# A two-layer hybrid decoder on one core: fifth product's copy in PSUM, later weights for the first pairs, x let go by halves, mixer products reordered

## Chip, cores and metric

One Trainium2 chip, one core of it. The metric is device time in microseconds (us) of one execution, as the median of several. Engines are named as the profile names them: PE (TensorE, matmul), PEld (its weight loads), DVE (VectorE), ACT (ScalarE), POOL (GpSimd), SP (SyncE, which issues nearly all DMAs here). PEclk is the granted clock of PE as a share of the full one.

## What is computed

All float32, one sequence of 512 tokens, width 1024, two layers. Cut to what the change touches:

```python
def swiglu_ffn(x, w_gu, w_down):                       # w_gu: 1024 x 5632, w_down: 2816 x 1024
    gate, up = jnp.split(x @ w_gu, 2, axis=-1)
    return (jax.nn.silu(gate) * up) @ w_down

def ab_mixer(xn, ...):                                 # layer 0's mixer
    proj = xn @ w_in
    xa, ga, qk, v, o, i_pre, f_pre = jnp.split(proj, cuts, axis=-1)
    ya = gelu(ga) * rglru(causal_dwconv(xa), ...)      # a linear scan over time
    yb = mlstm_block(qk, v, o, i_pre, f_pre, ...)      # 4 heads, 4 chunks of 128 tokens
    return concat([ya, yb]) @ w_out

for i in range(2):
    x = x + 0.5 * swiglu_ffn(rmsnorm(x, ffn1_norm[i]), ...)
    x = x + (ab_mixer if i == 0 else nsa_mixer)(rmsnorm(x, mix_norm[i]), ...)
    x = x + 0.5 * swiglu_ffn(rmsnorm(x, ffn2_norm[i]), ...)
return rmsnorm(x, final_norm)
```

## The kernel before

Six stages follow one another: f0a, ab, f0b, f1a, nsa, f1b (four feed-forward layers, two mixers). Features lie on partitions and the 512 tokens in the free direction. A float32 product is made of three matmuls in a rounded format (`mm3`, L175 to L177): weights and data are each split in a high part (written by ACT) and a low part (by DVE, now and then POOL), and PE does high·high, high·low, low·high. Raw weights come by DMA from SP's queue, which takes its DMAs in order.

**A feed-forward stage** makes 22 column tiles of gate and up. The first four (`CLASSIC`, j = 0 to 3) are done in the plain way, on the normalised input x, 8 slices k of 128 rows by `mm3`. x lies in four blocks: the high parts of k 0 to 3, the high parts of k 4 to 7, and the two blocks of low parts. The other tiles come as pairs (`Pair`): seven products p1 to p7 (each 4 slices, 12 matmuls of 256 columns) of combined weight quarters with combined quarters of x, named B11, Q7, Q6, B21, Q4, Q5, B22, in place of eight. `Quarters.split` makes them (L258 and L261 on ACT, L259 and L262 on DVE). The last four go into the blocks that x held, so their splits wait until the plain tile j = 3 has read x for the last time: `lay` says which quarter lies where. The first two pairs p and q run p.p1, p.p7, p.p6, q.p1, q.p7, p.p2, p.p4, p.p5, q.p6, p.p3, q.p2, q.p4, q.p5 on PE. `Pair.load` asks for four raw weight pieces (L305 to L308), adds them up on DVE (L309 to L311) and splits them (L318 on ACT, L319 on DVE).

Two accumulators a and b of a pair lie in PSUM. ACT copies p1's result into b's first half (L336); p5's is copied to an SBUF tile u4 (L363) and added by DVE (L364).

**What sets the order.** The build gives each instruction a place in its engine's list, and the engine takes the list in order; `tc.high_priority(offset=...)` moves instructions so many places ahead. Pieces of a pair are asked for RAHEAD = 400 places ahead and split SAHEAD = 230 ahead. PE's order in a feed-forward stage is written out by hand (`manual_schedule`).

**The mixer ab** runs four rounds i: projection and convolution for RG-LRU (`rg_conv`, L522 to L525), q and k of the mLSTM, RG-LRU's gate products (`rg_gate`, L539), the output gate; in between the mLSTM's gate rows (`gate_rows`, DVE work on 4 rows) and their transposes (`gate_cols`). Then `rg_scan`: reciprocals (L549), a scan (L554) for each i on DVE. Then v's projection (`proj_tok`), then four chunks of the mLSTM, each with scores in PSUM (L639 and L640), exponentials, and products L662, L664, L671.

Of the kernel before, what the change touches and what calls it, by code (L numbers as in the profile page):

```python
# [7 lines left out]
F32 = mybir.dt.float32  # L8
F32R = mybir.dt.float32r
AF = mybir.ActivationFunctionType  # L10
OP = mybir.AluOpType

P = 128
# [10 lines left out]
AHEAD = 90  # L24
SAHEAD = 230
RAHEAD = 400
EV = 320
H = T // 2
CLASSIC = 4
# [25 lines left out]
def build(tc, a, out, stages=("f0a", "ab", "f0b", "f1a", "nsa", "f1b")):  # L55
    nc = tc.nc
    with ExitStack() as ctx:
# [236 lines left out]
        class Pair:  # L294
# [1 line left out]
            def __init__(self, Q, down):  # L296
                self.Q, self.down, self.W = Q, down, {}

            def load(self, w, rb):
                with tc.high_priority(offset=RAHEAD):  # L300
                    ra, rc = (blk(rb[2 * (turns[1] % 2) + i], F32, f"r{i}")[:, :4 * T]
                              .rearrange("p (s c) -> p s c", s=4) for i in range(2))
                    turns[1] += 1

                    nc.sync.dma_start(ra[:, 0], w[0][:, :T])  # L305
                    nc.sync.dma_start(rc[:, 3], w[1][:, :T])
                    nc.sync.dma_start(ra[:, 3], w[1][:, T:])
                    nc.sync.dma_start(rc[:, 0], w[0][:, T:])  # L308
                    nc.vector.tensor_add(ra[:, 1:3], ra[:, 0:4:3], rc[:, 3:4].to_broadcast([P, 2, T]))  # L309
                    nc.vector.tensor_add(rc[:, 1], ra[:, 0], ra[:, 2])  # L310
                    nc.vector.tensor_add(rc[:, 2], rc[:, 0], rc[:, 1])  # L311
                with tc.high_priority(offset=SAHEAD):
                    for src, names in ((ra[:, 0:2], ("B11", "Q7")), (rc[:, 0:2], ("B21", "Q6")),
                                       (ra[:, 2:4], ("Q5", "Q4")), (rc[:, 2:3], ("B22",))):
                        hi, lo = parts()
                        m = len(names) * T
                        src = src.rearrange("p s c -> p (s c)")
                        nc.scalar.activation(hi[:, :m], src, AF.Copy)  # L318
                        nc.vector.tensor_sub(lo[:, :m], src, hi[:, :m].bitcast(F32))  # L319
                        for n, name in enumerate(names):  # L320
                            self.W[name] = hi[:, n * T:(n + 1) * T], lo[:, n * T:(n + 1) * T]
                return self
# [35 lines left out]

            def p5(self):
                self.product(self.a, "Q5", False)  # L360
                u4 = tp.tile([P, H], F32, name="u4", bufs=1)
                with tc.high_priority(offset=EV):
                    nc.scalar.activation(u4, self.a[:, :H], AF.Copy)  # L363
                    nc.vector.tensor_add(self.t2[:, H:], u4, self.t2[:, H:])  # L364

            def p3(self):
                self.product(self.a, "B22", False)
# [6 lines left out]
        def ffn(gname, wgu, wd, x, lay, nxt, first=None):  # L374
# [30 lines left out]
            for j in range(CLASSIC):  # L405
                (gh, gl), (uh, ul) = first if first and j == 0 else (wload(wgu[j, 0]), wload(wgu[j, 1]))
                pg, pu = psum(), psum2()
                seq = [(k, w) for k in range(KT) for w in range(2)]
                if j:
                    seq.sort(key=lambda e: e[1])  # L410
                with tc.manual_schedule(engines=PE_ONLY):
                    for n, (k, w) in enumerate(seq):
                        ks = slice(k * P, (k + 1) * P)
                        ps, hi, lo = ((pg, gh, gl), (pu, uh, ul))[w]
                        mm3(ps, hi[:, ks], lo[:, ks], x[0][k], x[1][k], k == 0, k == KT - 1)
                        if 16 * j + n == at[0]:
                            rms_sum([acc])
                        if 16 * j + n == at[1]:
                            rms_row()
                wait.append((j, pg, pu))  # L420
                if j == 1:
                    hidden(*wait.pop(0))
                    quarters.norm()
                    hidden(*wait.pop(0))
                    quarters.before()
                if j >= 2:
                    hidden(*wait.pop(0))
# [4 lines left out]
            while j0 < JT:  # L432
                j1 = min(JT, j0 + NH)
                js = list(range(max(CLASSIC, j0), j1))
                with tc.manual_schedule(engines=PE_ONLY):
                    if js[0] == CLASSIC:

                        p, q = (Pair(quarters.Q, downs(j)).load(wgu[j], rb) for j in js[:2])
                        for f in (p.p1, p.p7, p.p6, q.p1, q.p7, p.p2, p.p4, p.p5, q.p6, p.p3, q.p2, q.p4, q.p5):
                            f()  # L440
                        left = [q.p3]
                        js = js[2:]
                    for j in js:
                        p = Pair(quarters.Q, downs(j)).load(wgu[j], rb)
                        end = j == j1 - 1
                        for f in (p.p1, p.p7, *left, p.p6, p.p2, *((p.p5, p.p4, p.p3) if end else (p.p4, p.p5))):
                            f()
                        left = [] if end else [p.p3]
                if j1 == JT:
                    roots(hpart(JT - 1)[0].bitcast(F32))  # L450
                for i in range(KT):
                    ps = psum()
                    hi, lo = wload(wd[i, :, j0 * P:j1 * P], (j1 - j0) * P)
                    for k in range(j1 - j0):
                        mm3(ps, hi[:, k * P:(k + 1) * P], lo[:, k * P:(k + 1) * P], *hpart(k),
                            k == 0, k == j1 - j0 - 1)
                    nc.vector.scalar_tensor_tensor(X[i], ps, 0.5, X[i], op0=OP.mult, op1=OP.add)  # L457
                    if j1 == JT:
                        nxt(i)
                j0 = j1  # L460
# [15 lines left out]
        def ab(x, nxt):  # L476
# [83 lines left out]
            O4 = ones[0:4, 0:1].to_broadcast([4, T])  # L560
            gcol = cp.tile([P, NT, 8], F32, name="gcol")

            def gate_rows():
                ps = fm(x, "ab_fm", 4)
                nc.vector.tensor_mul(LI, ps[0:4], R[0:4])
                nc.vector.tensor_scalar(LI, LI, col("ml_b_i", rows=4), None, op0=OP.add)
                nc.vector.tensor_mul(Z, ps[32:36], R[32:36])
                nc.vector.tensor_scalar(Z, Z, col("ml_b_f", rows=4), None, op0=OP.add)
                nc.vector.scalar_tensor_tensor(E_, Z, -1.0, Z, op0=OP.mult, op1=OP.max)
                nc.scalar.activation(E_, E_, AF.Exp, scale=-1.0)  # L570
                nc.vector.tensor_scalar(Bc, E_, 1.0, None, op0=OP.add)
                nc.scalar.activation(LF, Bc, AF.Ln)
                nc.vector.tensor_scalar(Bc, Bc, -1.0, None, op0=OP.add)
                nc.vector.tensor_sub(E_, E_, Bc)
                nc.vector.tensor_add(LF, LF, E_)
                nc.vector.scalar_tensor_tensor(LF, Z, 0.0, LF, op0=OP.min, op1=OP.subtract)
                nc.vector.tensor_tensor_scan(Bc, O4, LF, 0.0, op0=OP.mult, op1=OP.add)
                nc.vector.tensor_sub(G, LI, Bc)
                nc.vector.tensor_tensor_scan(M, O4, G, -BIG, op0=OP.mult, op1=OP.max)
                nc.vector.tensor_add(EM, Bc, M)  # L580
                nc.scalar.activation(EM, EM, AF.Exp, scale=-1.0)
# [32 lines left out]
                nc.vector.tensor_sub(yal[i], z, yah[i].bitcast(F32))  # L614

            ahead(x, "ab_fm", (4, 0, 5, 9))
            gate_rows()
            for i in range(4):
                rg_conv(i)
                qk(i)  # L620
                qk(4 + i)
                rg_gate(i)
                out_gate(i)
                if i == 1:
                    gate_cols()

            rg_scan()
            pss = proj_tok(a["ab_v"], x)
# [6 lines left out]
            for c in range(NT):  # L635
                cs = slice(c * P, (c + 1) * P)
                pm, pst, pk = psum(), psum(), psum2()
                for h in range(NH):
                    nc.tensor.matmul(h4(pm)[:, h], sel[h], M[:, cs], start=True, stop=True)  # L639
                    nc.tensor.matmul(h4(pst)[:, h], kT[:, h, cs], qT[:, h, cs], start=True, stop=True)  # L640
                Et, Pt, kw, qd = (h4(t[b + c % 2]) for t, b in ((EP, 0), (EP, 2), (KQ, 0), (KQ, 2)))
                nc.vector.tensor_add(Et, h4(pm), mask.unsqueeze(1).to_broadcast([P, NH, P]))
                prev = mlast
# [502 lines left out]
        for n, st in enumerate(stages):  # L1146
# [13 lines left out]
            if st == "ab":  # L1160
                ab(x, nxt)
            elif st == "nsa":
                nsa(x, nxt)
            else:
                f = {"f0a": 0, "f0b": 1, "f1a": 2, "f1b": 3}[st]

                lay = (((4, 5, 6, 0, 1, 2, 3), (7, 8, 9, 10), (13, 14, 15, 16), (11, 12)) if base == 0 else
                       ((14, 15, 16, 4, 5, 6, 7), (2, 3, 0, 1), (8, 9, 10, 11), (12, 13)))
                ffn(plan[st], a["wgu"][f], a["wd"][f], x, lay, nxt, first if n == 0 else None)
            base = nbase  # L1170
            x = xn[0] if xn else None
# [101 lines left out]
```

## Time and profile before

| | |
|---|---|
| runs | 2098.58, 2088.83, 2093.01 us; median 2093.01 |
| the profiled execution | 2106.2 us; span of its records 2104.5 us; mean PEclk 0.976 |
| busy shares | PE 96%, PEld 83%, DVE 66%, ACT 49%, POOL 13% |
| chain that ended last, by engine | PE 72%, DVE 12%, DMA 6%, issue 5%, ACT 3% |

An engine's list is in order, so an instruction that waits holds all behind it. In a timeline row "[2.36 <-ACT qQ L261]" says that the engine sat idle for 2.36 us before the instruction until ACT's line 261, which writes qQ, let it go. A matmul's duration overlaps the next one's: from start to start is what it takes of PE.

### The profile page before, as it was taken

The page shows a single profiled execution, that of the slowest core. Times are in us where ns is not written, and L with a number is a line of the kernel's source. Part 1 is how long each engine was busy: PE and PEld are TensorE (multiplying, and loading weights), DVE is VectorE, ACT ScalarE, POOL GpSimd, SP SyncE. Part 2 cuts the span into 40 slices and gives each one's busy share as a digit, 9 for nine tenths or more (in the row PEclk, how much of TensorE's full clock was granted, in tenths as well). Part 3 has the DMA queues.
Part 4 walks back from the last instruction along what each step waited for, and adds up shares of the span by engine and source line. Part 5 has one row for each costly group of instructions (what it writes and reads, how often), then busy time and mean ns, then how long its engine had stood idle before and what let it go on. Part 6 is the DMA issues. An engine that isn't in the chain of part 4 may idle for free.

```text
span 2104.5 us, 30561 instructions
## 1 busy us (share of the span) xinstructions
PE 2014.4 (96%) x11896; PEld 1750.7 (83%) x11896; DVE 1383.4 (66%) x2189; ACT 1027.8 (49%) x1900; POOL 280.0 (13%) x290
## 2 busy tenths in 40 slices
PE   7999899989999999999999999999999999999997
PEld 5889898767888998897889989877777677999896
DVE  6847647488568657475865747433777788657474
ACT  4525436445445435254544525424877755435252
POOL 3000000243020000002000000201646440000002
PEclk9999999999899999999999999999999999999998
DMA  5232322222132323233232323321000032323212
GB/s 172 74 115 83 111 85 76 90 81 90 61 101 80 109 82 111 76 98 108 79 113 83 107 88 99 121 90 60 31 21 17 31 106 80 102 89 111 85 61 85
DMA packets 74737, 182.10 MB, mean 87 GB/s; under 512 B 8416, under 2 KB 9184, under 8 KB 74592
## 3 DMA queue, kind: packets, MB, share of 16 engines
q1 hardware_dynamic: 74448, 180.06, 27.6%
q8 instruction: 93, 1.52, 0.3%
q14 instruction: 52, 0.43, 0.1%
q10 hardware_dynamic: 144, 0.09, 0.0%
HBM read 178.02 MB, written 2.10 MB: 86 GB/s over the span
## 4 chain that ended last, share of the span: by engine, by line
PE 72%; DVE 12%; DMA 6%; issue 5%; ACT 3%; POOL 0%; SPq 0%; DVEq 0%; POOLq 0%; ACTq 0%
PE ps L175 17%; PE ps L176 17%; PE ps L177 17%; DMA r<-wgu 6%; PE pt L176 3%; PE pt L175 3%; PE pt L177 3%; PE px L984 2%; PE pt L779 2%; DVE wlo L319 1%; PE pt L1000 1%; DVE wx L319 1%; DVE r L309 1%; DVE r L310 1%; PE ps L944 1%
## 5 line engine op out<-in xcount | busy, mean ns | idle before, releaser
L169 ACT ACTIVATE whi<-raw 128x1024 fp32r<-128x1024 f32 (+2 forms) x196 | 193.3, 988 | 374.4 <-PE ps L176 254.5
L176 PE MATMUL ps<-h,whi 128*128 128x512 f32 x704 | 278.9, 396 | 0.7 <-DVE h L390 0.7
L175 PE MATMUL ps<-h,whi 128*128 128x512 f32 x704 | 277.8, 395 | 0.7 <-ACT h L389 0.7
L177 PE MATMUL ps<-h,wlo 128*128 128x512 f32 x704 | 277.2, 394 | 0.0
L318 ACT ACTIVATE whi<-r 128x1024 fp32r<-128x1024 f32 (+1 forms) x174 | 165.8, 953 | 211.2 <-PE ps L176 171.0
L170 DVE TENSOR_TENSOR wlo<-raw,whi 128x1024 fp32r<-128x1024 f32 (+2 forms) x166 | 192.5, 1162 | 78.7 <-ACT whi L169 73.8
L116 POOL TENSOR_TENSOR acc<-acc,t 128x512 f32<-128x512 f32 x48 | 76.9, 1603 | 1149.4 <-ACT t L114 1144.2
L457 DVE SCALAR_TENSOR_TENSOR X<-ps,X 128x512 f32<-128x512 f32 x96 | 66.4, 691 | 238.1 <-PE ps L177 238.1
L319 DVE TENSOR_TENSOR wlo<-r,whi 128x1024 fp32r<-128x1024 f32 (+1 forms) x174 | 189.1, 1088 | 28.1 <-ACT whi L318 27.8
L175 PE MATMUL ps<-x,whi 128*128 128x512 f32 x432 | 179.4, 415 | 6.0 <-ACT whi L1133 6.0
L176 PE MATMUL ps<-x,whi 128*128 128x512 f32 x432 | 171.0, 396 | 5.1 <-DVE x L105 4.9
L309 DVE TENSOR_TENSOR r<-r,r 128x1024 f32<-128x1024 f32 x72 | 89.4, 1242 | 130.5 <-DMA r<-wgu 130.4
L177 PE MATMUL ps<-x,wlo 128*128 128x512 f32 x432 | 171.3, 396 | 0.1
L175 PEld LDWEIGHTS ps<-h,whi 128*128 128x128 f32 x704 | 133.7, 190 | 30.8 <-ACT h L389 1.2
L176 PEld LDWEIGHTS ps<-h,whi 128*128 128x128 f32 x704 | 133.7, 190 | 30.7 <-DVE h L390 2.1
L177 PEld LDWEIGHTS ps<-h,wlo 128*128 128x128 f32 x704 | 133.7, 190 | 29.3
L175 PE MATMUL ps<-qB,whi 128*128 128x256 f32 x520 | 145.8, 280 | 2.8 <-ACT u L363 2.8
L177 PE MATMUL ps<-qB,wlo 128*128 128x256 f32 x520 | 145.2, 279 | 1.0 <-DVE wlo L319 1.0
L176 PE MATMUL ps<-qB,whi 128*128 128x256 f32 x520 | 145.3, 279 | 0.1
L319 DVE TENSOR_TENSOR wx<-r,wx 128x1024 fp32r<-128x1024 f32 (+1 forms) x114 | 125.1, 1098 | 23.6 <-ACT wx L318 21.1
L389 ACT ACTIVATE h<-t 128x512 fp32r<-128x512 f32 x88 | 55.4, 630 | 145.3 <-DVE t L371 143.1
L318 ACT ACTIVATE wx<-r 128x1024 fp32r<-128x1024 f32 (+1 forms) x114 | 107.5, 943 | 11.4 <-DVE r L309 9.1
(340 smaller groups left out, 5500.4 us busy)
## 6 DMA issues: line engine op xcount, KB each, us to landing
r<-wgu SPq DMA_DIRECT2D x288, 256.0 KB, 3.7
raw<-wd SPq DMA_DIRECT2D x64, 512.0 KB, 3.5
raw<-wgu SPq DMA_DIRECT2D x30, 512.0 KB, 3.6
raw<-wd SPq DMA_DIRECT2D x32, 384.0 KB, 3.1
raw<-ab_fm SPq DMA_DIRECT2D x21, 512.0 KB, 3.5
raw<-nsa_fm SPq DMA_DIRECT2D x17, 512.0 KB, 3.5
raw<-ab_out SPq DMA_DIRECT2D x8, 512.0 KB, 3.6
raw<-nsa_out SPq DMA_DIRECT2D x16, 256.0 KB, 2.7
```

The costliest lines, as they stand in the source:

```text
L116: nc.gpsimd.tensor_add(acc, acc, sq)
L169: nc.scalar.activation(hi[:, :n], raw[:, :n], AF.Copy)
L170: (eng or nc.vector).tensor_sub(lo[:, :n], raw[:, :n], hi[:, :n].bitcast(F32))
L175: nc.tensor.matmul(ps, wh, xh, start=start, stop=False, skip_group_check=on)
L176: nc.tensor.matmul(ps, wh, xl, start=False, stop=False, skip_group_check=on)
L177: nc.tensor.matmul(ps, wl, xh, start=False, stop=stop, skip_group_check=on)
L309: nc.vector.tensor_add(ra[:, 1:3], ra[:, 0:4:3], rc[:, 3:4].to_broadcast([P, 2, T]))
L318: nc.scalar.activation(hi[:, :m], src, AF.Copy)
L319: nc.vector.tensor_sub(lo[:, :m], src, hi[:, :m].bitcast(F32))
L389: nc.scalar.activation(hh, t2, AF.Copy)
L457: nc.vector.scalar_tensor_tensor(X[i], ps, 0.5, X[i], op0=OP.mult, op1=OP.add)
L779: nc.tensor.matmul(p2[m][:, :155].rearrange("p (g n) -> p g n", g=5), w[:, q * 256 + m * P:q * 256 + (m + 1) * P], tt[:, :, n:n + 8 * 30 + ...
```

## The change

The fifth product's copy goes into the second half of accumulator b, in PSUM, and DVE adds from there. The first two pairs of a stage use RFIRST = 180 and SFIRST = 110 places. Q4 and Q5 change places in `lay` (Q4 now lies over x's low parts of k 0 to 3), and j = 3 runs gate and up for k 0 to 3, then gate and up for k 4 to 7. In the mixer `gate_rows` is cut in two, `rg_gate(i)` comes a round later, and the score products of a chunk are grouped by kind.

```diff
+SFIRST = 110
+RFIRST = 180
...
-            def load(self, w, rb):
-                with tc.high_priority(offset=RAHEAD):
+            def load(self, w, rb, first=False):
+                with tc.high_priority(offset=RFIRST if first else RAHEAD):
...
-                with tc.high_priority(offset=SAHEAD):
+                with tc.high_priority(offset=SFIRST if first else SAHEAD):
...
                 self.product(self.a, "Q5", False)
-                u4 = tp.tile([P, H], F32, name="u4", bufs=1)
                 with tc.high_priority(offset=EV):
-                    nc.scalar.activation(u4, self.a[:, :H], AF.Copy)
-                    nc.vector.tensor_add(self.t2[:, H:], u4, self.t2[:, H:])
+                    nc.scalar.activation(self.b[:, H:], self.a[:, :H], AF.Copy)
+                    nc.vector.tensor_add(self.t2[:, H:], self.b[:, H:], self.t2[:, H:])
...
                 if j:
-                    seq.sort(key=lambda e: e[1])
+                    seq.sort(key=lambda e: (e[0] // 4 if j == CLASSIC - 1 else 0, e[1]))
...
-                        p, q = (Pair(quarters.Q, downs(j)).load(wgu[j], rb) for j in js[:2])
+                        p, q = (Pair(quarters.Q, downs(j)).load(wgu[j], rb, True) for j in js[:2])
...
-            def gate_rows():
+            def gate_in():
                 ps = fm(x, "ab_fm", 4)
                 nc.vector.tensor_mul(LI, ps[0:4], R[0:4])
+                nc.vector.tensor_mul(Z, ps[32:36], R[32:36])
+
+            def gate_rows():
...
-            gate_rows()
             for i in range(4):
                 rg_conv(i)
+                if i == 0:
+                    gate_in()
                 qk(i)
                 qk(4 + i)
-                rg_gate(i)
+                if i == 0:
+                    gate_rows()
+                else:
+                    rg_gate(i - 1)
                 out_gate(i)
                 if i == 1:
                     gate_cols()
+            rg_gate(3)
...
-                for h in range(NH):
-                    nc.tensor.matmul(h4(pm)[:, h], sel[h], M[:, cs], start=True, stop=True)
-                    nc.tensor.matmul(h4(pst)[:, h], kT[:, h, cs], qT[:, h, cs], start=True, stop=True)
+                with tc.manual_schedule(engines=PE_ONLY):
+                    for h in range(NH):
+                        nc.tensor.matmul(h4(pm)[:, h], sel[h], M[:, cs], start=True, stop=True)
+                    for h in range(NH):
+                        nc.tensor.matmul(h4(pst)[:, h], kT[:, h, cs], qT[:, h, cs], start=True, stop=True)
...
-                lay = (((4, 5, 6, 0, 1, 2, 3), (7, 8, 9, 10), (13, 14, 15, 16), (11, 12)) if base == 0 else
-                       ((14, 15, 16, 4, 5, 6, 7), (2, 3, 0, 1), (8, 9, 10, 11), (12, 13)))
+                lay = (((4, 5, 6, 0, 2, 1, 3), (7, 8, 9, 10), (13, 14, 15, 16), (11, 12)) if base == 0 else
+                       ((14, 15, 16, 4, 6, 5, 7), (2, 3, 0, 1), (8, 9, 10, 11), (12, 13)))
```

**SP at the very start of the program (stage f0a).** r are the raw weight pieces of the first two pairs, X the input's slices, raw the plain tiles' weights. Before:

```order
L305 DMA r_522<-wgu 128x512
L305 DMA r_546<-wgu 128x512
L306 DMA r_547<-wgu 128x512
L306 DMA r_523<-wgu 128x512
L307 DMA r_546<-wgu 128x512
L307 DMA r_522<-wgu 128x512
L308 DMA r_547<-wgu 128x512
L308 DMA r_523<-wgu 128x512
L1140 DMA X_70<-xT 128x512
L1132 DMA raw<-wgu 128x128 x2
L1132 DMA raw<-wgu 128x384 x2
L1137 DMA X_71<-xT 128x512
```

After:

```order
L1147 DMA X_75<-xT 128x512
L1147 DMA X_76<-xT 128x512
L1147 DMA X_77<-xT 128x512
L163 DMA raw<-wgu 128x1024 x2
L307 DMA r_546<-wgu 128x512
L307 DMA r_522<-wgu 128x512
L308 DMA r_523<-wgu 128x512
L308 DMA r_547<-wgu 128x512
L163 DMA raw<-wgu 128x1024
L309 DMA r_522<-wgu 128x512
L309 DMA r_546<-wgu 128x512
L310 DMA r_547<-wgu 128x512
```

The eight r loads that stood ahead of X now stand behind all of X and the weights of j = 1 (four of them) and behind a further plain weight (the other four, rows that follow). In the other stages SP's order is as before but for one pair of neighbours.

**ACT in stage f0b, between j = 3 and p.p2.** qB21, qQ4, qQ5, qB22 are the quarters that lie over x; the copies L336 and L347 are those behind p.p1 and p.p7, L341 that behind p.p2. Before:

```order
L261 ACTIVATE qQ5_5499<-xn9_5315 128x1024
L258 ACTIVATE qB21_5492<-xn10_5316 128x1024
L318 ACTIVATE whi_5540<-r0_5531 128x1024
L258 ACTIVATE qB22_5503<-xn10_5316 128x1024
L336 ACTIVATE ps_5555<-ps_5554 128x256
L318 ACTIVATE whi_5544<-r1_5532 128x1024
L347 ACTIVATE t2_5571<-pt_5570 128x256
L389 ACTIVATE h8_5416<-t2_5485 128x512
L352 ACTIVATE t2_5571<-ps_5554 128x256
L336 ACTIVATE ps_5599<-ps_5598 128x256
L318 ACTIVATE whi_5750<-r0_5741 128x1024
L347 ACTIVATE t2_5615<-pt_5614 128x256
L341 ACTIVATE t1_5556<-ps_5555 128x256
L318 ACTIVATE wx3_5548<-r0_5531 128x1024
L261 ACTIVATE qQ4_5496<-xn10_5316 128x1024
```

After (L260 and L263 are L258 and L261 of before, L338, L349, L354 are L336, L347, L352):

```order
L260 ACTIVATE qB21_5486<-xn10_5310 128x1024
L390 ACTIVATE h8_5410<-t2_5405 128x512
L320 ACTIVATE whi_5521<-r1_5503 128x512
L398 ACTIVATE t1_5478<-t1_5478 128x512
L320 ACTIVATE whi_5534<-r0_5525 128x1024
L263 ACTIVATE qQ4_5490<-xn10_5310 128x1024
L338 ACTIVATE ps_5549<-ps_5548 128x256
L390 ACTIVATE h8_5410<-t2_5479 128x512
L263 ACTIVATE qQ5_5493<-xn9_5309 128x1024
L349 ACTIVATE t2_5565<-pt_5564 128x256
L320 ACTIVATE whi_5538<-r1_5526 128x1024
L354 ACTIVATE t2_5565<-ps_5548 128x256
L260 ACTIVATE qB22_5497<-xn10_5310 128x1024
```

qQ4's split was the last of the four, behind p.p2's Silu and three more weight splits; it now stands second, ahead of p.p1's copy. On DVE its low part moves up likewise. f1b and f1a have the same move. In f0a the list of before stays as it was around qQ4 (it still stands behind p.p2's Silu).

**PE in the mixer, first score products.** Before:

```order
L639 MATMUL ps<-misc,ident 128x128
L640 MATMUL ps<-qT,kT 128x128
L639 MATMUL ps<-misc,ident 128x128
L640 MATMUL ps<-qT,kT 128x128
L639 MATMUL ps<-misc,ident 128x128
L640 MATMUL ps<-qT,kT 128x128
L639 MATMUL ps<-misc,ident 128x128
L640 MATMUL ps<-qT,kT 128x128
L656 MATMUL pt<-ident,kT 128x128 x4
L639 MATMUL ps<-misc,ident 128x128
```

After (L648 and L650 are L639 and L640, L666 is L656, L672 is L662):

```order
L648 MATMUL ps<-misc,ident 128x128 x4
L650 MATMUL ps<-qT,kT 128x128 x4
L666 MATMUL pt<-ident,kT 128x128 x4
L648 MATMUL ps<-misc,ident 128x128 x4
L650 MATMUL ps<-qT,kT 128x128 x4
L648 MATMUL ps<-misc,ident 128x128 x4
L650 MATMUL ps<-qT,kT 128x128
L672 MATMUL pt<-v_3523,ep_3527 128x129 x4
```

Sixteen of each kind alternated; they now run in fours where the program has them together. Further up in the mixer each gate product L539 stands one round (60 to 105 rows of PE) later than before, and on DVE all four reciprocals and all four scans now stand behind the last convolution's first steps, where two of each stood ahead of the k convolution of round 3.

## Rows read from the trace of the kernel before

**Rows 1.** page, head and section 1: span; busy time and its share by engine.

```profile
span 2104.5 us, 30561 instructions
PE 2014.4 (96%) x11896; PEld 1750.7 (83%) x11896; DVE 1383.4 (66%) x2189; ACT 1027.8 (49%) x1900; POOL 280.0 (13%) x290
```

**Rows 2.** waits of PE, 0 to 66.4: total, times, longest.

```profile
PE ps L175 <- ACT whi L1133: 6.0, 1, 6.0
PE ps L176 <- DVE x L105: 4.9, 3, 1.7
```

**Rows 3.** timeline, PE, start: start, us, engine, line [idle before <-releaser].

```profile
1.53 4.63 PE L1122 MATMUL ps<-ident 128*128 128x128 f32 x20 [1.53 <-POOL ident L94]
```

**Rows 4.** timeline, SP, start.

```profile
4.57 0.43 SPq L1140 DMA_DIRECT2D X<-xT  x1
```

**Rows 5.** timeline, DVE, start.

```profile
12.05 1.29 DVE L311 TENSOR_TENSOR r<-r 128x512 f32<-128x512 f32 x2
```

**Rows 6.** timeline, PE, stage f0b, from p.p2 to the start of p.p3.

```profile
675.96 0.28 PE L175 MATMUL ps<-qB,wx 128*128 128x256 f32 x1
...
679.93 0.58 PE L175 MATMUL pt<-qQ,wx 128*128 128x256 f32 x1 [2.36 <-ACT qQ L261]
...
681.71 0.58 PE L176 MATMUL pt<-qQ,wx 128*128 128x256 f32 x1 [1.20 <-DVE qQ L262]
...
688.12 0.28 PE L175 MATMUL ps<-qB,whi 128*128 128x256 f32 x1
...
688.24 0.28 PE L176 MATMUL ps<-qB,whi 128*128 128x256 f32 x1
```

**Rows 7.** timeline, PE, stage f1b, from p.p2 to p.p3.

```profile
1781.21 0.28 PE L175 MATMUL ps<-qB,whi 128*128 128x256 f32 x1
...
1793.84 0.28 PE L175 MATMUL ps<-qB,wx 128*128 128x256 f32 x1
```

**Rows 8.** timeline, PE, stage f0a, p.p4.

```profile
78.45 0.39 PE L175 MATMUL pt<-qQ,whi 128*128 128x256 f32 x1 [3.57 <-ACT qQ L261]
```

**Rows 9.** source views of four lines: count, ns min/median/max, first and last start.

```profile
L363 ACT ACTIVATE u<-ps x72: 359/367/386, 86.0 to 2051.3; 128x256 f32<-128x256 f32 x72
...
L336 ACT ACTIVATE ps<-ps x72: 364/368/379, 68.4 to 2044.2; 128x256 f32<-128x256 f32 x72
...
L364 DVE TENSOR_TENSOR t<-u,t x72: 414/418/526, 86.7 to 2051.7; 128x256 f32<-128x256 f32 x72
...
L357 DVE TENSOR_TENSOR t<-pt,t x72: 414/418/426, 83.1 to 2052.7; 128x256 f32<-128x256 f32 x72
```

**Rows 10.** timeline, PE, mixer, second gate product.

```profile
438.73 2.05 PE L539 MATMUL pt<-rg,num 128*128 128x512 f32 x2 [7.42 <-DVE rg L525]
```

**Rows 11.** windows of the mixer: length, busy of each engine, clock, DMA.

```profile
438.00:450.00 12.00, 11.27 (x39) 7.62 (x40) 9.69 (x9) 6.35 (x9) 5.14 (x3) 0.74 0.29 89
483.50:521.20 37.70, 37.70 (x161) 29.41 (x160) 36.42 (x38) 20.71 (x26) 10.13 (x6) 1.00 0.26 83
524.00:545.00 21.00, 21.00 (x74) 16.63 (x74) 5.58 (x11) 7.19 (x25) 0.00 (x0) 0.50 0.07 26
```

**Rows 12.** source views of RG-LRU's reciprocals and scans.

```profile
L549 DVE RECIPROCAL rg<-rg x4: 3341/3341/3347, 473.5 to 508.4; 128x512 f32<-128x512 f32 x4
...
L554 DVE TENSOR_TENSOR_SCAN hs<-rg,rg x4: 1206/2252/3410, 486.9 to 517.9; 128x512 f32<-128x512 f32 x4
```

**Rows 13.** timeline, DVE and POOL, late scan of the mixer.

```profile
512.69 3.41 DVE L554 TENSOR_TENSOR_SCAN hs<-rg,rg 128x512 f32<-128x512 f32 x1
...
512.19 2.83 POOL L170 TENSOR_TENSOR wlo<-raw,whi 128x1024 fp32r<-128x1024 f32 x1 [7.63 <-ACT whi L169]
```

**Rows 14.** timeline, PE, first score pass and first product of chunk 0.

```profile
519.42 0.48 PE L639 MATMUL ps<-misc,ident 4*128 4x128 f32 x2
...
534.95 1.93 PE L662 MATMUL pt<-v,ep 128*128 128x129 f32 x8
```

**Rows 15.** timeline, ACT, weights of f0a's first pair.

```profile
60.92 1.06 ACT L318 ACTIVATE whi<-r 128x1024 fp32r<-128x1024 f32 x1 [3.48 <-PE ps L176]
```

More of the change, by code (lines that the diff above doesn't have):

```diff
@@ L561, in ab @@
             gcol = cp.tile([P, NT, 8], F32, name="gcol")
-            def gate_rows():
+            def gate_in():
                 ps = fm(x, "ab_fm", 4)
                 nc.vector.tensor_mul(LI, ps[0:4], R[0:4])
+                nc.vector.tensor_mul(Z, ps[32:36], R[32:36])
+            def gate_rows():
                 nc.vector.tensor_scalar(LI, LI, col("ml_b_i", rows=4), None, op0=OP.add)
-                nc.vector.tensor_mul(Z, ps[32:36], R[32:36])
                 nc.vector.tensor_scalar(Z, Z, col("ml_b_f", rows=4), None, op0=OP.add)
```

## The prediction

> **What bounds the kernel now.** I read the head of the page first: PE is busy 2014.4 of 2104.5 us [rows 1], so only stretches where PE stands idle or runs at its lower clock can be shortened by reordering. PE's waits and timeline, read next stage by stage, leave three places that this diff touches. (1) The start: before its first plain matmul PE waits 6.0 us for a weight's high part on ACT, and then 4.9 us in three waits for low parts of x on DVE [rows 2]. (2) The first p4 of a feed-forward stage: in f0b it stands 2.36 us for ACT's qQ4 and 1.20 us for DVE's [rows 6]. (3) The mixer: a gate product waits 7.42 us for DVE [rows 10], and a stretch of 21 us runs at a clock of 0.50 [rows 11].
>
> **The fifth product's copy.** 72 copies on ACT change their target, 72 adds on DVE change one operand from SBUF to PSUM. Both new forms stand in the trace: ACT from PSUM to PSUM takes 368 ns against 367 to SBUF (L336, L363), DVE with a PSUM operand 418 against 418 (L357, L364) [rows 9]. The time is the same, and both engines have room under PE. b is held no longer than p2 to p3 hold it already. I take 0; the bounds are the spread of those medians, 72 times 1 ns, far below 1 us either way.
> [...]
>
> **The start of f0a.** SP issues eight r loads before the first slice of X, which is asked for at 4.57 us [rows 4]; after, X is first. DVE works on r until 13.34 (12.05 plus 1.29, [rows 5]) ahead of x's low parts; after, these adds stand behind all of x. PE cannot begin before its 20 start-up matmuls end, at 6.16 (1.53 plus 4.63, [rows 3]). So up to 6.0 us of the first wait and up to 4.9 us of the three others can go: at most 10.9. The first goes if X lands about 4.5 us earlier, as it is asked for that much earlier with nothing ahead; ACT's own split and DVE's follow at once. The 4.9 go only in part: x's eight low parts and the last plain low parts (POOL makes some) still follow one another while PE eats a slice in six matmuls. I take 2 of 4.9.
> What is late next: the four last r loads now stand behind a plain weight that waits for its slot, DVE reaches the first r add before they have landed, and behind that add on DVE's list stands the low part of j = 1's up weights. PE needs that only after all of gate of j = 1, so some 3 us of it are covered; without that cover up to 4 us come back. Sum 6 + 2 = 8 us; bounds 10.9, and 4 (only the first wait goes, 2 of it paid back at the r add). The r splits leave the start, but the first pair needs them only after four plain tiles.
>
> **x by halves, Q4 and Q5 exchanged.** From p.p2's start to p.p3's start PE does four products of 12 matmuls. One matmul is 0.12 us from start to start (688.12, 688.24), which is 5.7 us for four; it took 12.16 [rows 6], so 6.5 are lost: 3.56 of waits, and the rest because PE went on at its lower clock after them. In f1b the same stretch took 12.63 [rows 7]: 7.0 lost. f1a shows no stall of that size and is taken at nothing. After, qQ4's split on ACT stands ahead of p.p1's copy instead of behind p.p2's Silu and three weight splits, and the block under it is free after half of j = 3, so both parts are done some products before p4. What comes later is the split of B22, now the last of the four, behind p6's copy: p.p3 stands two products after p4, and I leave 0.5 us a stage for it. Gain 6.0 + 6.5, say 12; bounds 6 (half of the idle comes back at p5 or p.p3, and with it the clock) and 14 (nothing comes back).
> In f0a p4 waits 3.57 us for the same split [rows 8], but there ACT's list around it is unchanged: I take no gain.
>
> **The mixer.** Each gate product stands a round later on PE, and the mLSTM's gate rows on DVE behind the first convolution. The 7.42 us wait [rows 10] goes, and with it the low clock that follows it: the 12 us from 438 ran at a mean of 0.74 [rows 11], or 12 x 0.26 = 3.1 us lost. Of these 10.5 I leave 1 for a new wait, of the gate rows' transposes for their DVE chain: PE comes to the scores at about 519.4 - 9.5 = 510 ([rows 14] for the 519.4).
> But the scores' first use is a DVE add behind all four scans, and these have not come earlier. In 483.5 to 521.2 DVE was busy 36.42 of 37.70 us [rows 11], with the last convolution and the scans. After, two reciprocals of 3.34 [rows 12] and their companions, done earlier before, join this heap (about 9 us), and some 7 us of the convolution leave it because PE is ahead. So about 38 us, starting near 482: the scans end at about 520. The four scans took 1.21 to 3.41 us each [rows 12]; with all at one end or the other the heap ends 4 us earlier or later, 516 to 524. Chunk 0 then needs two mask adds, its exponentials and one product, three operations on 128x512 of 0.7 us and ACT between, 3 us by estimate: its first product on PE, L662 at 534.95 before [rows 14], comes at about 523 (519 to 527). Before, it was PE itself that was late, with 24 score products that alternate at half clock. I take 13 for the whole stage, near the 12 of this one place, since grouping also spares a little in the scores left; bounds 8 and 19.
> The 3.41 us scan at 512.69 ran while POOL had an L170 from 512.19 to 515.02 [rows 13]. [...]
>
> **Sum.** 0 + 8 + 12 + 13 = 33 us. The profiled execution took 2106.2, its span 2104.5; it would come to about 2073. It lies 13 us above the median of the three runs shown, 2093.01, and the gains are in PE's time in either; so the median comes to 2060. Adding the lower bounds gives 18, the upper 44: 2049 to 2075.
>
> **Rivals.**
> (a) The mixer gives its gain back. DVE's heap of scans is longer than I take it, PE waits for it before chunk 0 and drops to its lower clock, and the mLSTM ends where it did. For it: DVE's 36.42 of 37.70 us [rows 11]. Against: PE was the late one before. Gain 8 + 12 = 20: 2073.
> (b) The start gives nothing. PE begins at 6.2, but the r adds wait for their loads, and plain low parts queue behind them on DVE. For it: DVE's list is in order, and the loads are asked for after X and three plain weights. Against: 2 MB fewer in front of X. Gain 12 + 13 = 25: 2068.
> (c) The edits do what they say on the lists, and not on PE: the p4 wait moves to p5 or p.p3, since Q5 and B22 are still freed only at j = 3's end, and (a) holds as well. Gain at most 8: 2085, no change that can be told.
> (d) Slower. j = 3's gate weights are now in use until three quarters of that tile instead of half. ACT's split of the first pair's weights into that slot already waits for PE: 3.48 us at 60.92 in f0a [rows 15]. If it comes so late that p.p1 and p.p7 stand in all four stages, each stand is like that at p4, waits and lower clock, 6.5 to 7 us [rows 6, 7]. 4 x 7 = 28 takes most of the 33; it decides the sign from 33 / 4 = 8.3 us a stage, and at 11 the median is 2104. Against: a quarter of the tile, 12 matmuls of 512 columns, is left for one split of about 1 us on ACT and one on DVE.
>
> **How the numbers follow.** The sum as worked out, 0.62; (a) 0.15; (b) 0.10; (c) 0.09; (d) 0.04. 0.5% is 10.5 us, about what a measurement of this kernel can tell from no change. The sum, (a) and (b) are faster by more: 0.87; (c) same: 0.09; (d) slower: 0.04. The range takes the bounds of the sum, (a) and (b), and a little more at either end for terms that miss together: 2044 to 2078.
>
> **What would show it.** First plain matmul near 6.5 us instead of 12.17, and p1 of f0a 4 to 11 us earlier; no wait for qQ4 in f0b and f1b, and p.p3 some 6 us after p.p2; the wait of 7.42 at the second gate product gone, L662 (L672 after) of chunk 0 following the last scan on DVE by some 3 us, with PE waiting for it; DVE and ACT rows of p5 unchanged in length. The prediction is wrong if PE shows new waits at p.p1 or at p5 in several stages, if DVE stands long at the first r add with plain weights behind it, or if the mLSTM ends where it did.

## The result, and the profile after

The changed kernel takes 2073.13 us (median of 6 runs, 2064.37 to 2077.04) against 2094.05 for the kernel before (6 runs): ratio 0.9892, 95% interval 0.9865 to 0.9920, or 22.6 us faster (17 to 28). A second set of runs on the chip gave 2068.05 against 2098.64: 0.9861 (0.9841 to 0.9882), 29 us. The forecast was 2060 and 33 us. The profiled execution took 2072.72, its span is 2071.0, which is 33.5 under the profiled execution of before; why that difference flatters the change is told below.

The start of f0a after the change, timeline of PE:

```profile
5.49 0.48 PE L177 MATMUL ps<-x,whi 128*128 128x512 f32 x1
...
17.09 0.50 PE L179 MATMUL pt<-x,wlo 128*128 128x512 f32 x1 [2.02 <-POOL wlo L1144]
...
30.01 0.50 PE L179 MATMUL pt<-x,wlo 128*128 128x512 f32 x1 [0.82 <-DVE wlo L172]
...
33.91 1.16 PE L152 MATMUL pt<-ident,Rcol 128*128 128x128 f32 x8 [1.32 <-DVE Rcol L133]
```

and that of DVE there:

```profile
26.46 2.36 DVE L311 TENSOR_TENSOR r<-r,r 128x1024 f32<-128x1024 f32 x2 [8.35 <-DMA r<-wgu]
```

The first plain matmul runs at 5.49 instead of 12.17: the wait of 6.0 us [rows 2] is gone. In place of the 4.9 us of waits for x's low parts stand others, for a high part of x (0.91), for POOL, for a weight's low part behind the r add, and for the row factors: PE's idle gaps from 6 to 40 us sum to 5.7. DVE stands 8.35 us at the first r add. p1 of f0a comes at 59.64 instead of 66.39.

The four late quarters in f0b (p.p2, p.p4, p.p3), in f1b (p.p2, p.p3) and f0a's p.p4, timeline of PE:

```profile
663.48 0.28 PE L177 MATMUL ps<-qB,wx 128*128 128x256 f32 x1
...
664.84 0.28 PE L177 MATMUL pt<-qQ,wx 128*128 128x256 f32 x1
...
669.09 0.28 PE L177 MATMUL ps<-qB,whi 128*128 128x256 f32 x1
```

```profile
1753.74 0.28 PE L177 MATMUL ps<-qB,whi 128*128 128x256 f32 x1
...
1759.42 0.28 PE L177 MATMUL ps<-qB,wx 128*128 128x256 f32 x1
```

```profile
72.35 0.38 PE L177 MATMUL pt<-qQ,whi 128*128 128x256 f32 x1 [3.90 <-ACT qQ L263]
```

From p.p2 to p.p3 it is 5.61 us in f0b instead of 12.16 [rows 6], and 5.68 in f1b instead of 12.63 [rows 7]; f0a's wait is there as before [rows 8].

The fifth product's copy and add, source views:

```profile
L364 ACT ACTIVATE ps<-ps x72: 362/368/378, 79.6 to 2018.2; 128x256 f32<-128x256 f32 x72
L365 DVE TENSOR_TENSOR t<-ps,t x72: 411/417/425, 80.0 to 2018.6; 128x256 f32<-128x256 f32 x72
```

368 and 417 ns, against 367 and 418 [rows 9].

The mixer, timeline of PE at the gate rows' transposes, at the scores and at chunk 0's first product:

```profile
436.47 0.19 PE L590 MATMUL pt<-ident,misc 4*128 4x4 f32 x1 [2.21 <-DVE misc L581]
441.73 0.27 PE L591 MATMUL pt<-ident,misc 4*128 4x4 f32 x1 [5.07 <-ACT misc L584]
...
515.64 1.15 PE L648 MATMUL ps<-misc,ident 4*128 4x128 f32 x8
516.73 1.16 PE L650 MATMUL ps<-qT,kT 128*128 128x128 f32 x8
...
522.93 0.46 PE L650 MATMUL ps<-qT,kT 128*128 128x128 f32 x2 [1.36 <-DVE mlast L655]
524.81 2.09 PE L672 MATMUL pt<-v,ep 128*128 128x129 f32 x8 [1.42 <-DVE ep L663]
```

and windows of the changed kernel (columns as in [rows 11]):

```profile
436.00:448.00 12.00, 6.46 (x26) 5.35 (x27) 9.11 (x12) 5.92 (x7) 3.31 (x3) 0.72 0.26 89
...
515.60:520.60 5.00, 5.00 (x38) 4.43 (x38) 4.97 (x5) 2.95 (x4) 3.21 (x2) 1.00 0.30 105
520.60:530.60 10.00, 7.22 (x36) 6.72 (x35) 6.30 (x13) 6.42 (x23) 0.00 (x0) 0.67 0.15 52
530.60:540.60 10.00, 10.00 (x73) 8.94 (x73) 6.28 (x16) 4.74 (x16) 0.00 (x0) 0.99 0.01 2
```

The 7.42 us wait [rows 10] is gone from the gate product, but 2.21 and 5.07 us stand at the transposes now, with a clock of 0.72 around them, like the 0.74 before [rows 11]. Chunk 0's product follows DVE at 524.81, as reckoned, but the stretch of the scores itself reads quite otherwise than before: a clock of 1.00, 0.67, 0.99. These are the same stretches, from the first score on, in the kernel before:

```profile
519.40:524.40 5.00, 5.00 (x24) 3.58 (x23) 2.56 (x3) 4.16 (x8) 3.54 (x2) 0.84 0.36 110
524.40:534.40 10.00, 10.00 (x29) 6.86 (x29) 2.65 (x5) 1.75 (x7) 0.00 (x0) 0.50 0.13 50
534.40:544.40 10.00, 10.00 (x42) 9.00 (x42) 2.74 (x5) 4.66 (x17) 0.00 (x0) 0.50 0.01 2
```

### The profile page after: what moved, and what is told of

Read it like the earlier page. It is cut to its first block, busy times and chain, and to the rows that moved or that the text cites. A ratio compares the mean times of both kernels' runs of the same rounds, so it can differ in the third digit from the quotient of the medians.

```text
span 2071.0 us, 30532 instructions
## 1 busy us (share of the span) xinstructions
PE 1991.6 (96%) x11896; PEld 1735.3 (84%) x11896; DVE 1373.8 (66%) x2189; ACT 1028.7 (50%) x1900; POOL 278.0 (13%) x290
## 4 chain that ended last, share of the span: by engine, by line
PE 60%; DVE 9%; DMA 4%; issue 3%; ACT 2%; POOL 0%; SPq 0%; POOLq 0%; DVEq 0%; ACTq 0%
PE ps L177 14%; PE ps L178 14%; PE ps L179 14%; DMA r<-wgu 3%; PE pt L179 3%; PE pt L177 3%; PE pt L178 3%; PE px L994 2%; PE pt L789 2%; PE pt L1010 1%; DVE wx L321 1%; PE ps L954 1%; PE pt L1011 1%; DVE wlo L172 1%; DVE wlo L321 1%
## 5 line engine op out<-in xcount | busy, mean ns | idle before, releaser
L458 DVE SCALAR_TENSOR_TENSOR X<-ps,X 128x512 f32<-128x512 f32 x96 | 66.4, 691 | 231.0 <-PE ps L179 231.0
```

## Experiments

Each was timed beside runs of the kernel before on the same chip; differences below are its ratio's, with the 95% interval's half width. The parts are named start (RFIRST, SFIRST), quarters (exchange of Q4 and Q5 and j = 3 by halves), mixer (gate edit and grouped scores) and fifth product.

**The four parts alone.** Each is the kernel before with only the lines of that part in the diff above.

Start:

> The kernel before with the late weights of the first two pairs alone (RFIRST, SFIRST). Theory: p1 of f0a comes about 6.7 us earlier (66.4 before, 59.6 in the changed kernel), and what is gained there stays: 6 to 7 us faster in all. Rival: the pairs that follow in f0a are paced by the arrival of weights, so the stage ends where it did: p1 6.7 us earlier, but the end of f0a and the whole within 2 us of before.

Measured: 0.9954, 9.6 us faster (± 3.8). In this profile p1 of f0a comes at 59.6, and f0a ends 7.8 us earlier: what is gained there stays. The theory holds.

Quarters:

> The kernel before with Q4 and Q5 exchanged and j = 3 by halves alone. Theory: 6 us in f0b and 6.5 in f1b, nothing in f1a and f0a, 12 to 13 us faster in all. Rival: B22's later split or the gate weights' later release gives half of it back: 6 us.

Measured: 0.9929, 14.9 us (± 3.7). The first group of pairs of f0b and that of f1b (from p.p1 to the first down product) are each 6.3 us shorter, and f0a's p4 waits as before. The theory holds.

Mixer:

> The kernel before with the mixer's reordering alone (gate rows, gate products, grouped scores). Theory: the stage is 11 us shorter, as between the two traces (1.7 us gained at its start, 12.5 at the start of f0b). Rival: that was the luck of one pair of runs, since a new wait of 7.3 us stands at the gate rows' transposes: 3 to 5 us.

Measured: 0.9946, 11.3 us (± 3.6). The sum of the part is that of the theory, and the rival's 3 to 5 us are outside the interval; which of its two edits brings it is for the runs below.

Fifth product:

> The kernel before with the fifth product's copy into PSUM alone. Theory: 0, within 2 us, the copy 368 ns and the add 418 as before. [...]

Measured: 0.9994, 1 us faster (± 4). No cost that can be told; 3 us slower is outside the interval.

The parts sum to 37 us, more than the whole's 22.6 or 29.

**The whole again, and the mixer taken apart.**

> The changed kernel again, for a second profile and more runs. Parts alone gave about 9.6 (start), 14.9 (quarters), 11.3 (mixer) and 1 (fifth product) us, 36 in sum, the whole 22.6. Theory: the parts overlap in the mixer, where the start alone and the quarters alone also gained 6 to 7 us without touching it; the whole then stays at 20 to 27 us. Rival: no overlap, the first runs of the whole were slow by chance: 31 to 38 us.

Measured: 0.9861, 29 us (± 4.3). It lies between the two and decides for neither. In this profile f0a ends 7.1 us earlier, not 1.7 as in the first profile, where PE's waits from p1 to that end sum to 15.2 us instead of 12.6. So one kernel's f0a differs by 5.4 us between two executions. Over all 14 profiles f0a ends at 397.8 to 404.0 in the seven with the start edit and at 404.3 to 406.9 in the seven without it; the means are 5.6 us apart.

```diff
-                for h in range(NH):
-                    nc.tensor.matmul(h4(pm)[:, h], sel[h], M[:, cs], start=True, stop=True)
-                    nc.tensor.matmul(h4(pst)[:, h], kT[:, h, cs], qT[:, h, cs], start=True, stop=True)
+                with tc.manual_schedule(engines=PE_ONLY):
+                    for h in range(NH):
+                        nc.tensor.matmul(h4(pm)[:, h], sel[h], M[:, cs], start=True, stop=True)
+                    for h in range(NH):
+                        nc.tensor.matmul(h4(pst)[:, h], kT[:, h, cs], qT[:, h, cs], start=True, stop=True)
```

> The kernel before with the score products grouped by kind, alone. Theory: the low clock after 521 us comes from the alternating score products; grouped they keep the clock, and 6 to 8 us of the stretch from 520 to 560 go. Rival: the clock falls for PE's waiting and not for the order: 0 to 2 us.

Measured: 0.9938, 13 us (± 4.5), as much as the whole mixer part and more than the theory's 6 to 8; the rival is out. Windows of this kernel, from the first score on, and two PE rows of its timeline (first score, first product of chunk 0):

```profile
519.10:524.10 5.00, 5.00 (x38) 4.43 (x38) 3.61 (x6) 4.52 (x10) 3.50 (x2) 1.00 0.39 111
524.10:534.10 10.00, 10.00 (x75) 8.91 (x76) 6.92 (x15) 6.31 (x24) 0.00 (x0) 1.00 0.14 51
534.10:544.10 10.00, 10.00 (x69) 9.03 (x68) 5.53 (x12) 3.62 (x12) 0.00 (x0) 1.00 0.20 56
```

```profile
519.14 1.15 PE L640 MATMUL ps<-misc,ident 4*128 4x128 f32 x8
...
525.33 1.06 PE L664 MATMUL pt<-v,ep 128*128 128x129 f32 x8
```

The clock is full throughout, and chunk 0's product comes 6.2 us after the first score; before it came 15.5 us after it [rows 14].

```diff
...
-            gate_rows()
             for i in range(4):
                 rg_conv(i)
+                if i == 0:
+                    gate_in()
                 qk(i)
                 qk(4 + i)
-                rg_gate(i)
+                if i == 0:
+                    gate_rows()
+                else:
+                    rg_gate(i - 1)
...
+            rg_gate(3)
```

> The kernel before with the gate rows cut in two and each gate product a round later, alone, scores as before. Theory: the wait of 7.4 us only changes its place to the gate rows' transposes (2.2 and 5.1 us in the changed kernel), so 0 to 3 us. Rival: the later scans and the wait's new place keep the clock, 6 us or more.

Measured: 0.9994, 1 us (± 4). Timeline of PE: the wait has moved and not gone; behind this one stands another, of 5.0 us, for ACT.

```profile
439.44 0.24 PE L589 MATMUL pt<-ident,misc 4*128 4x4 f32 x1 [2.32 <-DVE misc L580]
```

**Versions beyond the change.** The transposes a round later, in the changed kernel:

```diff
-                if i == 1:
+                if i == 2:
                     gate_cols()
```

> The changed kernel with the gate rows' transposes one round later (after round 2 in place of round 1). Theory: their wait of 7.3 us on DVE and ACT goes, and the low clock behind it, and the scores come that much earlier; but the scans on DVE, not PE, then hold chunk 0, so of some 9 us 2 to 5 remain against the changed kernel: 25 to 30 us faster than before. Rival: PE's time counts in full: 30 to 35 us.

Measured: 0.9847, 32 us (± 5) faster than before, and 3 us under the second set of runs of the whole, which these intervals do not tell apart, nor the theory from the rival. The wait at the transposes is gone. PE waits 3.2 and 1.1 us for DVE before chunk 0 instead, as the theory has it, and 3.9 us for a weight's low part on DVE at 435, which the theory does not have.

The gate edit taken back, the rest as changed (the diff above without its gate lines):

> The changed kernel with the gate rows and gate products back in their old places, scores grouped. Theory: the gate edit only moves the wait of 7.4 us and holds the scans back, so that PE stands for DVE before chunk 0 (1.4 + 1.1 us, clock 0.66 for 10 us after); without it the mixer is 217 us long as with the scores alone, against 221, and the whole 3 to 5 us faster than the changed kernel: 31 to 36 faster than before. Rival: the gate edit pays in the whole, and this is 3 us slower than the changed kernel or more.

Measured: 0.9848, 32 us (± 6); not told apart from the whole by time. By the traces the mixer (from its row factors' product to that of f0b) takes 216.9 us here, against 220.6 and 221.4 in the two profiles of the whole, and PE does not wait for DVE before chunk 0.

The gate rows behind round 1, the transposes behind round 2, with the gate rows cut in two as in the change (against the run before):

```diff
...
-            gate_rows()
+            gate_in()
             for i in range(4):
                 rg_conv(i)
                 qk(i)
                 qk(4 + i)
                 rg_gate(i)
                 out_gate(i)
                 if i == 1:
+                    gate_rows()
+                if i == 2:
                     gate_cols()
```

> As the run before, but the gate rows' DVE work behind round 1 and their transposes behind round 2, the gate products in their old places. Theory: the convolution of round 1 no longer stands behind the gate rows on DVE, so the wait of 7.4 us and the low clock after it go without holding the scans back: some 8 us more than the run before, less what DVE's list then lacks (it is nearly full from 483 us on): 3 to 8 us. Rival: DVE is the bound of the mixer, and nothing comes of it: 0 to 2 us.

Measured: 0.9852, 31 us (± 6). The wait of 7.4 us is gone, the mixer takes 213.6 us, 3.3 less; in time it doesn't show. PE's waits are smaller ones for the gate products (1.9 and 2.3 us) and for POOL (1.4).

The late quarters earlier in their lists:

```diff
-            quarters.after()
+            with tc.high_priority(offset=40):
+                quarters.after()
```

> As the run before, and the four late quarters asked for 40 places earlier. In f0a ACT's split of qQ4 then stands ahead of p.p2's Silu. Theory: the wait of 3.9 + 1.5 us at f0a's p4 and the low clock after it go, 5 to 8 us more than the run before. Rival: DVE, full there, makes other low parts late, and 0 to 2 us come of it.

Measured: 0.9840, 33.5 us (± 5), the fastest median of all, 2060.00, and not told apart from the three before it, so that theory and rival stay undecided by time. The wait of 3.9 us at f0a's p4 is not gone: it is 3.76 us long and has changed its name, to the copy behind p.p7, as PE's timeline shows. The second wait, of 1.5, is gone, and f0a's first two pairs take 24.0 us instead of 26.4; in f1b they take 1.2 us more.

```profile
71.75 0.58 PE L177 MATMUL pt<-qQ,whi 128*128 128x256 f32 x1 [3.76 <-ACT t L349]
```

**The exchange of Q4 and Q5 without j = 3 by halves.**

> The kernel before with Q4 and Q5 exchanged alone, j = 3 as before. Theory: the block under Q4 comes free only at three quarters of j = 3 and its split stands later on ACT (still ahead of p.p2's Silu in f0b), so part of the waits in f0b and f1b stays: 5 to 9 us of the 15 of both edits. Rival: the exchange does all of it, and p.p3 comes 5.7 us after p.p2 as with both: 12 us or more.

Measured: 0.9946, 11 us (± 5). By the trace p.p3 comes 6.8 us after p.p2 in f0b (12.16 before, [rows 6]; 5.61 with both), and the first group of pairs is 5.4 us shorter in f0b and 5.3 in f1b, against 6.3 each with both edits. The time lies between theory and rival and does not tell them apart. By the traces the exchange does 10.7 of the 12.6 us, more than the theory gave it, and j = 3 by halves the rest.

## Why the forecast came out as it did

**Sum.** The direction and the range were right. The size was a third too large against the first set of runs (33 against 22.6) and within the interval of the second (29 ± 4.3). Read stage by stage in the two profiles of the whole, the terms come to 25 and 30 us: f0a ends 1.7 and 7.1 us earlier (forecast 8), the first groups of pairs of f0b and f1b are 12.8 and 13.1 shorter (12), the mixer 10.8 and 10.0 (13).
That the two profiled spans differ by 33.5, almost the forecast, is luck, and the step "the gains are in PE's time in either" failed. The profiled execution of before, 2106.2, lies 12 us above its median of 2094. From the start of f0b's second group of pairs to that of f1a's last group of down products, where no term of the sum lies, it took 556.7 us; all 13 others profiled are shorter, by 3.5 to 11.5 us. The three with mixer edits alone (the whole part, grouped scores, gate edit), which leave this stretch as it was, are shorter by 3.5, 9.1 and 9.6. So of the 33.5 some 4 to 10 were that one execution's. Its mixer, 231.4 us, from which the mixer's term was read, is one of the longest as well: in the four other profiles without a mixer edit it took 224.5 to 231.4.

**Fifth product.** 0 forecast, 1 ± 4 measured, rows of 368 and 417 ns. That was right.

**Start.** Forecast 8, measured 6.8 and 7.5 at p1 of f0a in the two profiles of the whole, 9.6 ± 3.8 alone. The mechanism was right: X first, first plain matmul at 5.49. That is earlier than the 6.16 which the prediction took for the earliest, because it added a row's whole length, and that length reaches into the next product: after the change the row of the 20 start-up matmuls lasts from 1.53 to 5.73, and the next product begins at 5.49. Of the term "6 + 2" the 6 became 6.7, and the 2 became nothing, since POOL's low part and the row factors took the place of x's low parts. The wait at the r add came as forecast and is long on DVE (8.35) but costs PE 0.82; the r adds that follow stand between the row factors' steps on DVE, for which PE waits 1.32. How much of it is left at f0a's end differs from execution to execution, as said above.

**Quarters.** Forecast 12, measured 6.1 in f0b and 6.7 in f1b in the two traces, and 14.9 ± 3.7 alone. It was right in each step, f0a's unchanged wait too; PE does not wait for B22, for which 0.5 us was left. What I put down to both edits is for the most part the exchange's.

**Mixer.** Forecast 13, measured 10.8 and 10.0 between the traces and 11.3 ± 3.6 alone: the size came near, but by luck, since its steps were wrong. "Of these 10.5 I leave 1 for a new wait, of the gate rows' transposes": that wait is 7.3 us, and the low clock came with it (0.72 in the 12 us from 436), so that from the row factors on PE reached the scores only 0.5 to 2 us earlier with the gate edit, not 9.5. "Grouping also spares a little in the scores left": grouping alone gives 13 ± 4.5, the gate edit alone nothing (1 ± 4). The term of the scans was near, chunk 0 at 524.81 against 523, with PE waiting for DVE; but that wait is a cost that the gate edit brings, as the run without it shows.
Two things lie in grouping. The second score product before, and the first row behind the first eight after:

```profile
519.83 0.49 PE L640 MATMUL ps<-qT,kT 128*128 128x128 f32 x2
```

```profile
517.72 0.60 PE L666 MATMUL pt<-ident,kT 128*128 128x128 f32 x4
```

At full clock eight scores take 2.1 us in fours (515.64 to 517.72), where each took 0.41 alternating (519.42 [rows 14] to 519.83), with a clock of 1.00 in either stretch; that is 1.2 us for eight, and by estimate 3.6 for the 24 that alternate ahead of chunk 0's first product. And the clock stays: 0.84, 0.50, 0.50 in 25 us before is by estimate 10.8 us lost (each length times what its clock lacks to 1.00), grouped alone none. Together that is 14 us, as is the difference between the mixers of these two traces, 231.4 and 217.2 us.

**The parts' overlap.** Start alone and quarters alone had a mixer shorter by 6.9 and 5.5 us, though they don't touch it. The gate edit alone had one shorter by 5.9 us, and no gain in time. Windows of the start alone, from its first score:

```profile
510.90:515.90 5.00, 5.00 (x28) 3.62 (x27) 2.40 (x3) 4.24 (x8) 3.12 (x2) 1.00 0.34 111
515.90:525.90 10.00, 10.00 (x34) 7.51 (x34) 3.41 (x7) 2.04 (x8) 0.00 (x0) 0.54 0.14 49
525.90:535.90 10.00, 10.00 (x74) 8.95 (x73) 5.12 (x11) 5.77 (x21) 0.00 (x0) 0.95 0.01 2
```

The order is the alternating one of before, but the clock is low for 10 us instead of 24. Chunk 0's product came 15.5, 16.1 and 15.5 us after the first score in three profiles with alternating scores (before, fifth product, exchange), and 13.6, 11.4 and 11.4 in three others (start, quarters, gate). If the other executions are like these, what the grouped scores save is counted partly in the other parts alone, and their sum passes the whole by that; this is argued and not shown. With one profile for each of these kernels it stays open whether this goes with the kernel or with the execution.

**Rivals.** (a) came in its first half: DVE's heap of scans ended at 522, PE waited 1.36 and 1.42 us for DVE, and the clock was 0.67 for 10 us; but the mixer kept most of its gain. (b) came in part: the r add holds DVE, for 0.8 + 1.3 us of PE. (c) and (d) did not come: PE does not wait at p5, p.p3 or p.p1 of f0b and f1b.

## What to carry to other kernels

A wait on a long in-order chain that is moved, with its consumer merely further along the same chain, can be there again at the next consumer, as here 7.42 us at the gate product came back as 2.21 and 5.07 at the transposes: price the whole chain to the next use and not the wait that is seen. Before a gain is summed against a profiled execution, compare that execution with its median; stretches that are long in that one run alone belong to no edit. And an order that alternates two kinds of small matmuls is worth a run by itself: here it was the part of the diff that looked smallest, and alone it gave 13 us (± 4.5).

## What was not expected of the hardware

Before, PE's clock fell to 0.50 some 3 us after the first score and stayed there for 24 us, though the records show PE busy 10.00 of 10.00 us and no wait. Up to 534.95 these were 4-row and 128-row products of 128 columns, alternating; behind that, mostly products of 129 columns. In five profiled kernels with alternating scores (before, fifth product, start, quarters, gate edit) the clock fell there, 3 to 9 us after the first score and with no wait on record, and stayed low for 10 to 24 us: from 5 us after the first score its mean over the next two stretches of 10 us was 0.50 and 0.50 in the first two kernels, 0.54 and 0.95, 0.70 and 0.62, 0.69 and 0.63 in the others. With the products in fours and no wait it stayed at 1.00 in three profiles (grouped scores alone, the gate edit taken back, the gate rows behind round 1). In a fourth, that of the late quarters earlier in their lists, it fell all the same, for some 3.5 us:

```profile
515.80:518.80 3.00, 3.00 (x15) 3.00 (x15) 1.69 (x4) 2.04 (x7) 0.00 (x0) 0.50 0.37 142
```

So the order goes with how long the clock is low here, none or 3.5 us against 10 to 24, and does not by itself decide whether it falls. The trace of before shows PE idle at no time there, with 10.00 of 10.00 us busy; but its rows reach into one another (the first score's is 0.48 us long, the next begins 0.41 after it), and at a clock of 1.00 a product took 0.41 us alternating and 0.27 in fours, so it cannot rule out that PE stood still for moments within that. What brings the clock down in the alternating order is not shown.
